# A trunk of two hybrid layers: three first projections taken by quarters of the adaLN weights, and the first GLA head drawn into the end of the RG-LRU

## The chip, the cores and the metric

The kernel runs on one core of a Trainium2 chip. The time is the device time of one execution in microseconds; of several executions the median counts.

## The reference

Two layers act on 512 tokens of 1024 features: 256 context tokens and 256 latent tokens. Both kinds share all weights. Only the latent stream is returned, so the second layer computes context rows only where latent rows read them. Each layer is, cut to what matters here:

```
mod   = c_silu @ mod_w + mod_b                  (shift, scale, gate; two of each)
h     = rms_norm(x, norm1_g) * (1 + scale) + shift
lx, ly, gq, gk, gv, gr, gz, aq, ak, av, bg = split(h @ w_in)
y1 = RG-LRU: conv of lx, gates a and i by tanh, a recurrence in both directions, times gelu(ly)
y2 = GLA:    4 heads, chunks of 64 tokens, decays from gz, both directions, rms norm, times silu(gr)
y3 = GQA:    8 heads over 2 key heads, rotary embedding, softmax
m  = sum over the branches of sigmoid(bg) * (y @ w_branch);  x = x + gate1 * (m @ w_out)
x  = x + gate2 * (relu(modulated norm of x @ mlp_w1) ** 2 @ mlp_w2)
```

## The kernel before

Features lie on the 128 partitions, eight k tiles of 128 of them, and tokens along the free axis. A weight tile is 128x1024 fp32 (512 KB). SP loads it into one of three buffers (`wraw`, L194), ACT casts it to a high part `wh` (L200), and DVE subtracts to get a low part `wl` (L201). The activations are split likewise into `hh` and `hl` (tile `h`, `split_to`, L293 and L294). A GEMM (`gemm`, L252) is 24 matmuls (L212): for each k tile wh by hh, wh by hl, and wl by hh. It sums in one of four PSUM banks named `mm`. Four other banks, `mx`, serve the small matmuls. In layer 1 GEMMs whose output is needed for the latent tokens only have 256 columns in place of 512 (`c0` is 256 there).

The program is written as one sequence, and a scheduler decides each engine's order from it. `tc.high_priority(AHEAD)` lets a weight's load and its two splits go ahead of their place. Each engine then works strictly in its own order, and the tables `LYS`, `MG`, `GZP` and `G0P` say after which step a piece of another branch is written.

**Beginning** (L438 to L475). The first four blocks of 2 MB of mod_w are quarters: each gives shift and scale for two k tiles. `mod_load` fetches a quarter in 16 pieces of 1 KB per partition. `mod_half` multiplies it with the conditioning vector (32 matmuls of L212, `mx<-modw,cs`), copies (L307), transposes (L216) and adds the bias (`modT`, L319). `norm_apply` makes the factor (`amul`, L420), multiplies (L425 on POOL, L427 on DVE), applies (L432 on DVE, L434 on ACT) and splits. After that stand nineteen small operations for the constants of RG-LRU (L454 to L475). Then come the GEMMs of ly (`gate_y`, three of them first) and of lx (`lru_conv`).

**RG-LRU** takes the eight blocks in pairs, i = 0, 2, 4, 6. `lru_conv` has a GEMM and four taps (L512 on ACT, L515 on DVE). `lru_gates` has four fp32 matmuls (L526) and tanh on ACT (L527, L531), and `lru_decay` an exp (L538). A square root over the pair (L630) needs another table on ACT. `lru_scan` has the recurrences on DVE (L545 to L555) and a split. After the pair i = 2, `gla_z` loads and splits `wz` and computes the decays' low rank input (L568, L572). After the pair i = 6, `gla_gates(0)` computes the decays of GLA's head 0 (L598 on PE; L601, L604, L605 on ACT with two table loads; L602 to L612 on DVE).

**GLA** takes four heads one after the other (`gla`, L648). A head computes its gates, k (copied out at L653), q (L656), for every second head v of two heads in four PSUM banks (L661), then for each direction `dd` the decayed k and q (L677 to L710), the scores (L715, L717), transposes of k (L728) and the states (L741), then the output (L760), its norm (L762 to L767), and r (two GEMMs, L769 to L772), whose product with the transposed output (L775, L776) is y2. Four `merge` steps of the first branch follow head 1 and four follow head 2. Then come GQA (k is transposed at L851), the other merges, the output projection and the MLP.

Of the kernel before, what the change touches and what calls it, by code (L numbers as in the profile page):

```python
# [15 lines left out]
F32 = mybir.dt.float32  # L16
# [7 lines left out]
KT = 8  # L24
# [6 lines left out]
WSPB, EBB, G2B, WRB = 3, 1, 3, 3  # L31
NSPL = 5
WQ = 1
# [4 lines left out]
GZP, G0P = 2, 6  # L38
# [66 lines left out]
def trunk_kernel(ctx: ExitStack, tc: tile.TileContext, out: bass.AP, d: dict):  # L105
# [48 lines left out]
    c8 = const.tile([128, KT, 2], F32, name="c8")  # L154
# [9 lines left out]
    pick = const.tile([128, 2, 32], F32, name="pick")  # L164
    G.memset(pick, 0.0)
    for b in range(2):
        G.memset(pick[:, b, b:b + 1], 1.0)
# [6 lines left out]
    th = const.tile([128, KT, 2], F32, name="th")  # L174
# [146 lines left out]
    def mods(l, us, pace, nd=KT):  # L321
# [19 lines left out]
        for u, j in halves:  # L341
            bs = (0, 1) if l == 0 or u < 2 else (1,)
            acc = [tmp() for _ in bs]
            terms = [(pick[:, b, :], a) for a, b in zip(acc, bs)]
# [22 lines left out]
    def mod_load(l, u, h, tag):  # L367

        t = yp.tile([128, KT, 2, 256], F32, name="modw", tag=tag)
        src = d["mod_w"][l, u]  # L370
        if u < 2:
            nc.sync.dma_start(t, src.rearrange("p k (h c) -> p k h c", h=2)[:, :, :, 256 * h:256 * h + 256])
        else:
            nc.sync.dma_start(t.rearrange("p k h c -> p k (h c)"), src[:, :, 512 * h:512 * h + 512])
        return t

    def mod_half(l, u, h, t):
        dsts = (4 * u + 2 * h, 8 + 4 * u + 2 * h) if u < 2 else (8 * u + 4 * h, 8 * u + 4 * h + 2)
# [759 lines left out]
```

## Time and profile before

| | |
|---|---|
| median of 3 runs | 1898.92 us (1896.93 to 1903.13) |
| the profiled execution | 1897.52 us, of which the span is 1895.7 |
| mean granted clock of TensorE | 0.989 |
| busy: PE, DVE, ACT, POOL | 1810.9, 1282.9, 924.8, 57.1 us |
| DMA | 255.62 MB, 135 GB/s in the mean |

The page gives the busy time of each engine first, then the span in 40 slices, the queues, the chain that ended last and the costliest groups of instructions. PE's digit falls below 9 in three places: the first slice, the fourth (142 to 190 us) and the 28th and 29th (1280 to 1374 us). Those places are looked at with the timeline and the waits.

### The profile page before, as it was taken

What the parts mean: (1) busy time and instruction counts of PE and PEld (TensorE: products, weight loads), DVE (VectorE), ACT (ScalarE), POOL (GpSimd) and SP (SyncE); (2) the same over time, 40 slices, a digit from 0 to 9 for tenths busy, and PEclk for the clock granted to TensorE, in tenths of its full rate; (3) what the DMA queues carried; (4) which work ended last, traced back from release to release, by engine and by line L of the source; (5) the groups of instructions that cost most, each with busy time, mean ns of one, the idle gap of its engine ahead of it and who ended that gap; (6) DMA issues with size and microseconds to landing.
All of it is one profiled execution on the core that took longest, in us unless ns stands there. A gap on an engine that the chain in (4) does not pass through costs nothing.

```text
span 1895.7 us, 26828 instructions
## 1 busy us (share of the span) xinstructions
PE 1810.9 (96%) x10248; PEld 1509.6 (80%) x10248; DVE 1282.9 (68%) x2177; ACT 924.8 (49%) x1586; POOL 57.1 (3%) x88
## 2 busy tenths in 40 slices
PE   5998999999999999999999999996999999999999
PEld 4765778887777888988888889764888878998887
DVE  5677764535566767789744448787765668577877
ACT  3778544334434333564232325876654554455443
POOL 1000000000000000000000001000000000000000
PEclk9999999999999999999999999998999999999999
DMA  9322223222211566666633335531343333664664
GB/s 318 99 74 73 69 69 90 77 93 78 72 51 56 190 193 196 222 224 199 211 109 97 98 102 185 164 114 61 130 122 111 122 123 91 234 193 150 190 190 154
DMA packets 91617, 255.62 MB, mean 135 GB/s; under 512 B 9184, under 2 KB 20576, under 8 KB 91488
## 3 DMA queue, kind: packets, MB, share of 16 engines
q1 hardware_dynamic: 91488, 253.90, 42.6%
q8 instruction: 81, 1.33, 0.3%
q14 instruction: 48, 0.39, 0.1%
HBM read 252.82 MB, written 1.05 MB: 134 GB/s over the span
## 4 chain that ended last, share of the span: by engine, by line
issue 49%; PE 39%; DVE 5%; ACT 4%; POOL 2%; DMA 0%; SPq 0%; POOLq 0%; ACTq 0%; DVEq 0%
PE mm L212 31%; PE mx L212 2%; PE mx L760 1%; PE mx L741 1%; DVE wl L201 1%; ACT wh L200 1%; PE mx L715 1%; PE mx L526 1%; POOL t L425 1%; PE mx L216 1%; DVE lru L546 0%; PE mx L717 0%; DVE lru L545 0%; ACT lru L630 0%; ACT lru L527 0%
## 5 line engine op out<-in xcount | busy, mean ns | idle before, releaser
L212 PE MATMUL mm<-h,wh 128*128 128x512 f32 (+1 forms) x2640 | 733.3, 360 | 8.3 <-DVE wh L198 4.5
L200 ACT CAST wh<-wraw 128x1024 fp32r<-128x1024 f32 x363 | 379.8, 1049 | 544.3 <-PE mm L212 465.3
L201 DVE TENSOR_TENSOR wl<-wraw,wh 128x1024 fp32r<-128x1024 f32 x365 | 445.8, 1223 | 257.6 <-ACT wh L200 254.2
L212 PEld LDWEIGHTS mm<-h,wh 128*128 128x128 f32 x2640 | 468.3, 189 | 85.4 <-issue 6.6
L212 PE MATMUL mm<-h,wl 128*128 128x512 f32 (+1 forms) x1448 | 493.2, 341 | 0.0
L212 PEld LDWEIGHTS mm<-h,wl 128*128 128x128 f32 x1448 | 273.8, 189 | 31.9 <-issue 1.4
L212 PE MATMUL mm<-yh,wh 128*128 128x512 f32 (+1 forms) x640 | 224.7, 351 | 2.4 <-DVE big L957 2.4
L212 PE MATMUL mm<-yh,wl 128*128 128x512 f32 (+1 forms) x640 | 224.3, 350 | 0.0
L212 PE MATMUL mm<-yl,wh 128*128 128x512 f32 (+1 forms) x640 | 222.6, 348 | 0.0
L212 PE MATMUL mm<-wh,h 128*128 128x512 f32 x576 | 187.3, 400 | 18.5 <-ACT t L653 18.1
L212 PE MATMUL mm<-yp,wh 128*128 128x256 f32 (+1 forms) x704 | 186.0, 338 | 3.8 <-ACT g L787 2.3
L212 PE MATMUL mm<-yp,wl 128*128 128x256 f32 x512 | 144.4, 282 | 0.0
L356 DVE SCALAR_TENSOR_TENSOR t<-t,cs,t 128x512 f32<-128x512 f32 x178 | 127.2, 746 | 24.1 <-DMA t<-mod_w 15.1
L212 PEld LDWEIGHTS mm<-wh,h 128*128 128x128 f32 x576 | 109.7, 191 | 42.3 <-ACT t L653 18.9
L212 PEld LDWEIGHTS mm<-yp,wh 128*128 128x128 f32 x704 | 120.8, 191 | 20.1 <-ACT g L787 2.5
L212 PEld LDWEIGHTS mm<-yh,wh 128*128 128x128 f32 x640 | 121.6, 190 | 17.8 <-issue 3.4
L212 PEld LDWEIGHTS mm<-yh,wl 128*128 128x128 f32 x640 | 121.2, 189 | 15.3 <-issue 0.7
L212 PEld LDWEIGHTS mm<-yl,wh 128*128 128x128 f32 x640 | 121.2, 189 | 15.0 <-issue 0.5
L212 PE MATMUL mm<-wl,h 128*128 128x512 f32 x288 | 115.2, 400 | 2.0 <-DVE wl L201 2.0
L212 PEld LDWEIGHTS mm<-yp,wl 128*128 128x128 f32 x512 | 97.1, 190 | 1.0 <-issue 1.0
L212 PE MATMUL mx<-t,t 128*128 128x128 f32 (+2 forms) x416 | 81.8, 338 | 0.0
L957 DVE SCALAR_TENSOR_TENSOR big<-mm,modT,big 128x256 f32<-128x256 f32 x64 | 28.6, 480 | 66.8 <-PE mm L212 66.8
(226 smaller groups left out, 1987.4 us busy)
## 6 DMA issues: line engine op xcount, KB each, us to landing
wraw<-wt SPq DMA_DIRECT2D x365, 512.0 KB, 3.6
t<-mod_w SPq DMA_DIRECT2D x144, 256.0 KB, 3.8
modw<-mod_w SPq DMA_DIRECT2D x6, 2048.0 KB, 14.1
big<-xt SPq DMA_DIRECT2D x8, 512.0 KB, 5.3
gw<-lruw SPq DMA_DIRECT2D x16, 256.0 KB, 3.5
out<-big SPq DMA_DIRECT2D x8, 128.0 KB, 2.5
t<-glaw SPq DMA_DIRECT2D x8, 96.0 KB, 3.1
t<-ropeg SPq DMA_DIRECT2D x2, 256.0 KB, 3.0
```

Source lines behind the costliest of these rows:

```text
L200: S.copy(wh, r)
L201: (G if lo == "G" else V).tensor_tensor(wl, r, wh.bitcast(F32), op=ALU.subtract)
L212: P.matmul(o, a, b, **kw)
L216: P.transpose(o, a, ident)
L356: V.scalar_tensor_tensor(a, t, c, a, op0=ALU.mult, op1=ALU.add)
L425: G.tensor_tensor(h[:, :n], x[:, k, c0:c1], st[1][:, :n], op=ALU.mult)
L526: P.matmul(pg, gw[:, 2 * dd + q, :], xc, start=True, stop=True)
L715: P.matmul(psc[:, c], en[:, c], em[:, c], start=True, stop=True)
L741: P.matmul(pu[:, :256], kt[:, 128 * t:128 * t + 128], v_[t], start=True, stop=True)
L760: P.matmul(po[:, :256], a, b, start=j == 0, stop=j == len(mm) - 1)
L957: V.scalar_tensor_tensor(x[:, i, c], ps[:, 256 * s - a:256 * s - a + 256], s0[:, i, s:s + 1], x[:, i, c], op0=ALU.mult, op1=ALU.add)
```

## The change

The four first quarters of mod_w (and the two that layer 1 loads at its end) are laid out on the host so that each is one row of 16 KB per partition, and the loads of the first two weights stand ahead of the third and after the first quarter. The first three ly projections (`first_gemm`) take the two k tiles of a quarter as soon as that quarter's norm is there, in three PSUM banks at once, between the multiplications of the next quarter. Their high parts are all cast by ACT. The RG-LRU constants are computed in `gate_consts` after the first `lru_conv`, in place where they can be. `wz` is loaded and split ahead of the RG-LRU loop, into the pool `g2`, which has four buffers in place of three.

In the last RG-LRU pair head 0's k and q GEMMs (`gla_kq`) come before the gates of block 6, and its decays and v (`gla_gates`, `gla_v`) between the gates of block 6 and of block 7. Its r GEMMs (`gla_r`) come before the last scans. For the other heads k and q come first, then the deferred end of the head before (`end`, transposes and product), then v and r. A head's state matmuls follow the k transposes of both directions. The end of head 3 comes after the attention's k and v projection.

```diff
...
-WSPB, EBB, G2B, WRB = 3, 1, 3, 3
+WSPB, EBB, G2B, WRB = 3, 1, 4, 3
...
-GZP, G0P = 2, 6
+GZP = 2
...
-                nc.sync.dma_start(t, d["mod_w"][l, u][:, k, 512 * j:512 * j + 512])
+                nc.sync.dma_start(t, d["mod_w"][l, u, j][:, k, :])
...
-        src = d["mod_w"][l, u]
-        if u < 2:
-            nc.sync.dma_start(t, src.rearrange("p k (h c) -> p k h c", h=2)[:, :, :, 256 * h:256 * h + 256])
-        else:
-            nc.sync.dma_start(t.rearrange("p k h c -> p k (h c)"), src[:, :, 512 * h:512 * h + 512])
+        nc.sync.dma_start(t, d["mod_w"][l, u, h].rearrange("p k (h c) -> p k h c", h=2))
...
-    mq = [mod_load(0, q // 2, q % 2, ("yh", "yl")[q % 2]) for q in range(WQ)]
-    first = [weight(0, "in", O_LY + 128 * i, hi="V", ahead=0) for i in range(2)]
-    mq += [mod_load(0, q // 2, q % 2, ("yh", "yl")[q % 2]) for q in range(WQ, 4)]
+    first = [weight(0, "in", O_LY + 128 * i, ahead=0) for i in range(2)]
+    mq = [mod_load(0, 0, 0, "yh")]
+    first.append(weight(0, "in", O_LY + 256, ahead=0))
+    mq += [mod_load(0, q // 2, q % 2, ("yh", "yl")[q % 2]) for q in range(1, 4)]
+    first_ps = [ps_mm.tile([128, 512], F32, name="mm") for _ in range(3)]
+    def first_gemm(i, q):
+        wh, wl = (a.rearrange("p (k m) -> p k m", k=8) for a in first[i])
+        for k in range(2 * q, 2 * q + 2):
+            mm(first_ps[i], wh[:, k, :], hn1[0][:, k, :], start=k == 0, stop=False)
+            mm(first_ps[i], wh[:, k, :], hn1[1][:, k, :], start=False, stop=False)
+            mm(first_ps[i], wl[:, k, :], hn1[0][:, k, :], start=False, stop=k == KT - 1)
     st = norm_stats(x1, 0)
     for q in range(4):
-        mod_half(0, q // 2, q % 2, mq[q])
+        for i in range(2) if q else ():
+            first_gemm(i, q - 1)
+        g = mod_half(0, q // 2, q % 2, mq[q])
+        next(g)
+        if q:
+            first_gemm(2, q - 1)
+        run(g)
         norm_apply(0, 1, x1, 0, T, st, hn1, range(2 * q, 2 * q + 2))
+    for i in range(3):
+        first_gemm(i, 3)
...
-    lo_, hi_ = PCOLS["lam"]
-    V.tensor_copy(lam, par[:, :, lo_:hi_])
-    S.activation(la, lam, AF.Abs)
...
-    V.tensor_scalar(c2[:, :, 0, :], lam, -4.0, None, op0=ALU.mult)
-    V.tensor_scalar(c2[:, :, 1, :], lam, 2.0, None, op0=ALU.mult)
...
-    V.tensor_scalar(habx, par[:, :, lo_:hi_], 0.5, None, op0=ALU.mult)
+    habx = par[:, :, lo_:hi_]
+    def gate_consts():
...
+        S.activation(la, lam, AF.Abs)
...
+        V.tensor_scalar(habx, habx, 0.5, None, op0=ALU.mult)
...
         def gate_y(i):
-            w = first[i] if l == 0 and i < 2 else weight(l, "in", O_LY + 128 * i, hi=E_LYH)
-            ps = gemm(w, hh, hl, c0)
+            if l == 0 and i < 3:
+                ps = first_ps[i]
+            else:
+                ps = gemm(weight(l, "in", O_LY + 128 * i, hi=E_LYH), hh, hl, c0)
...
+        wz = tmp1(F32, (128, KT, 32))
+        nc.sync.dma_start(wz, d["wz"][l])
+        wzs = g2.tile([128, KT, 64], F32R, name="wzs", tag="g2")
+        split_to(wzs[:, :, :32], wzs[:, :, 32:], wz)
...
-            wz = tmp1(F32, (128, KT, 32))
-            nc.sync.dma_start(wz, d["wz"][l])
-            wzs = t2.tile([128, KT, 64], F32R, name="wzs", tag="t2")
-            split_to(wzs[:, :, :32], wzs[:, :, 32:], wz)
...
+        v2 = {}
+        def gla_kq(h):
...
+            pk = gemm(weight(l, "in", O_GK + 128 * h), hh, hl, 0)
+            k_ = tmp()
+            cp(E_K)(k_, pk)
+            pq = gemm(weight(l, "in", O_GQ + 128 * h), hh, hl, c0)
+            q_ = tmp()
+            S.activation(q_[:, c0:], pq, AF.Copy, scale=128.0 ** -0.5)
+            return k_, q_
...
+        def gla_v(h):
...
+                for t, ps in gemm_tok(l, O_GV + 256 * h, hh, hl, range(4)).items():
...
+            return [v2.pop((h, t)) for t in range(4)]
...
+        def gla_r(h):
+            ys = []
...
+                pr = gemm(weight(l, "in", O_GR + 256 * h + 128 * j), hh, hl, c0)
+                y = gtmp()
+                S.activation(y[:, c0:], pr, AF.Tanh, scale=0.5)
+                V.scalar_tensor_tensor(y[:, c0:], y[:, c0:], 1.0, pr, op0=ALU.add, op1=ALU.mult)
+                ys.append(y)
+            return ys
...
         lru_conv(0)
+        if l == 0:
+            gate_consts()
         for i in range(0, 8, 2):
             lru_conv(i + 1)
-            lru_gates(i)
             if i < 6:
+                lru_gates(i)
                 lru_conv(i + 2)
+            else:
+                kq0 = gla_kq(0)
+                lru_gates(i)
+                gates0 = gla_gates(0)
+                v0 = gla_v(0)
             lru_gates(i + 1)
...
+            if i == 6:
+                ys0 = gla_r(0)
             for j in range(2):
                 lru_scan(i + j)
             if i == GZP:
                 zs = gla_z()
-            if i == G0P:
-                gates0 = gla_gates(0)
...
+        def gla(h, before=None):
+            if h:
+                bs = gla_gates(h)
+                k_, q_ = gla_kq(h)
+                before()
+                v_ = gla_v(h)
+                ys = gla_r(h)
+            else:
+                bs, (k_, q_), v_, ys = gates0, kq0, v0, ys0
...
-                kt = tmp()
+                kt = gtmp()
...
+                kts.append((kt, decp))
+            for dd, (kt, decp) in enumerate(kts):
+                seq = (0, 1, 2, 3) if dd == 0 else (1, 0, 3, 2)
...
-            for j in range(2):
-                pr = gemm(weight(l, "in", O_GR + 256 * h + 128 * j), hh, hl, c0)
...
-                V.scalar_tensor_tensor(y[:, c0:], y[:, c0:], 1.0, pr, op0=ALU.add, op1=ALU.mult)
-                po = mx()
...
+            def end():
+                for j, y in enumerate(ys):
+                    po = mx()
+                    for t in range(t0, 4):
+                        P.transpose(po[:, 128 * t:128 * t + 128], on[t - t0][:, 128 * j:128 * j + 128], ident)
+                    V.scalar_tensor_tensor(y[:, c0:], po[:, c0:], hg[:, j:j + 1], y[:, c0:],
+                                           op0=ALU.mult, op1=ALU.mult)
+                    split_to(y2h[:, 2 * h + j, c0:], y2l[:, 2 * h + j, c0:], y[:, c0:])
+            return end
...
+        end = None
         for h in range(4):
-            gla(h)
+            end = gla(h, end)
...
             av.append(a)
+        end()
...
-    a["mod_w"] = np.ascontiguousarray(mw.reshape(NL, 8, 128, 6, 1024).transpose(0, 3, 2, 1, 4))
+    mw = mw.reshape(NL, 8, 128, 6, 2, 512).transpose(0, 3, 4, 2, 1, 5).copy()
+    m0 = mw[0, :2].reshape(2, 2, 128, 8, 2, 256)
+    mw[0, :2] = m0.transpose(0, 4, 2, 3, 1, 5).reshape(2, 2, 128, 8, 512)
+    a["mod_w"] = mw
```

In these excerpts of the engines' orders "L212 MATMUL mx<-modw,cs" and its like are the line, the operation, and output and inputs. The number behind a name tells tiles apart. "x32" counts equal instructions in a row.

PE at the beginning, from the first quarter's multiplication on. Before (mm_444, mm_471 and mm_504 are the three ly projections):

```order
L212 MATMUL mx_195<-modw_129,cs_98 32x128 x32
L216 MATMUL mx_230<-ident_94,t1_228 128x128
L212 MATMUL mx_247<-modw_143,cs_98 32x128 x32
L212 MATMUL mm_444<-h_128,wh_133 128x512 x2
L216 MATMUL mx_282<-ident_94,t1_280 128x128
L212 MATMUL mm_444<-h_128,wl_134 128x512
L212 MATMUL mm_444<-h_128,wh_133 128x512 x2
L212 MATMUL mm_444<-h_128,wl_134 128x512
L212 MATMUL mm_471<-h_128,wh_139 128x512 x2
L212 MATMUL mm_471<-h_128,wl_140 128x512
```

With the change (mm_154, mm_155 and mm_156 are the three):

```order
L210 MATMUL mx_203<-modw_140,cs_98 32x128 x32
L214 MATMUL mx_238<-ident_94,t1_236 128x128
L210 MATMUL mm_154<-h_127,wh_130 128x512 x2
L210 MATMUL mm_154<-h_127,wl_131 128x512
L210 MATMUL mm_154<-h_127,wh_130 128x512 x2
L210 MATMUL mm_154<-h_127,wl_131 128x512
L210 MATMUL mm_155<-h_127,wh_136 128x512 x2
L210 MATMUL mm_155<-h_127,wl_137 128x512
L210 MATMUL mm_155<-h_127,wh_136 128x512 x2
L210 MATMUL mm_155<-h_127,wl_137 128x512
L210 MATMUL mx_267<-modw_148,cs_98 32x128 x32
L210 MATMUL mm_156<-h_127,wh_144 128x512 x2
```

The second quarter's multiplication stood ahead of the first projection, and now stands behind twelve matmuls of two projections.

ACT in layer 0 from the last exp of RG-LRU on, before (L630 is the square root, L601 to L605 are head 0's decays, L653 and L656 copy k and q):

```order
L538 ACTIVATE lru<-lru,c_403 128x512 x2
L630 ACT_TABLE_LOAD
L630 ACTIVATE lru<-lru,epsc 128x2048
L601 ACTIVATE eb<-mx,par 128x512 x2
L604 ACT_TABLE_LOAD
L604 ACTIVATE eb<-eb 128x1024
L605 ACT_TABLE_LOAD
L605 ACTIVATE eb<-eb 128x1024
L293 CAST yh<-lru 128x512
L653 COPY t_1323<-mm 128x512
L656 ACTIVATE t_1356<-mm 128x512
```

With the change, from block 6's gates on (L544 and L548 are tanh, L555 the exp of RG-LRU; L620 to L624 are head 0's decays):

```order
L544 ACTIVATE lru<-mx,par 128x512 x2
L548 ACTIVATE lru<-lru,c_483 128x512
L544 ACTIVATE lru<-mx,par 128x512 x2
L548 ACTIVATE lru<-lru,c_483 128x512
L620 ACTIVATE eb<-mx,par 128x512 x2
L555 ACT_TABLE_LOAD
L555 ACTIVATE lru<-lru,c_483 128x512
L623 ACTIVATE eb<-eb 128x1024
L198 CAST wh<-wraw 128x1024
L624 ACT_TABLE_LOAD
L624 ACTIVATE eb<-eb 128x1024
L555 ACT_TABLE_LOAD
```

The copy of k stood behind the square root, the decays and a split that takes the scan's result. Now the decays stand ahead of the square root, between the exps of blocks 6 and 7.

DVE in layer 1 at the scans of the last pair, before (L545 to L555):

```order
L545 SCALAR_TENSOR_TENSOR lru<-lru 128x512 x2
L546 TENSOR_TENSOR lru<-lru 128x512 x2
L548 SCALAR_TENSOR_TENSOR lru<-lru 128x512
L550 SCALAR_TENSOR_TENSOR lru<-lru 128x256
L545 SCALAR_TENSOR_TENSOR lru<-lru 128x512
L551 SCALAR_TENSOR_TENSOR lru<-lru 128x256
L546 TENSOR_TENSOR lru<-lru 128x512
L554 TENSOR_TENSOR lru<-lru 128x256
L548 SCALAR_TENSOR_TENSOR lru<-lru 128x512
L555 TENSOR_TENSOR lru<-lru,big 128x256
L545 SCALAR_TENSOR_TENSOR lru<-lru 128x512
L294 TENSOR_TENSOR yp<-lru,yp 128x256
```

With the change (the scans are L562 to L572, L199 splits weights, L663 is r's product):

```order
L562 SCALAR_TENSOR_TENSOR lru<-lru 128x512 x2
L199 TENSOR_TENSOR wl<-wraw,wh 128x1024
L563 TENSOR_TENSOR lru<-lru 128x512
L663 SCALAR_TENSOR_TENSOR g_10999<-g_10999,mm 128x256
L663 SCALAR_TENSOR_TENSOR g_11033<-g_11033,mm 128x256
L565 SCALAR_TENSOR_TENSOR lru<-lru 128x512
L199 TENSOR_TENSOR wl<-wraw,wh 128x1024
L563 TENSOR_TENSOR lru<-lru 128x512
L562 SCALAR_TENSOR_TENSOR lru<-lru 128x512
L567 SCALAR_TENSOR_TENSOR lru<-lru 128x256
L563 TENSOR_TENSOR lru<-lru 128x512
L199 TENSOR_TENSOR wl<-wraw,wh 128x1024
```

Weight splits and r's product now stand between the scans, where none stood before.

## Rows read from the trace of the kernel before

**Rows 1.** The page: busy time of each engine (share of the span) and instructions.
```profile
PE 1810.9 (96%) x10248; PEld 1509.6 (80%) x10248; DVE 1282.9 (68%) x2177; ACT 924.8 (49%) x1586; POOL 57.1 (3%) x88
```

**Rows 2.** Windows; columns: PE, PEld, DVE, ACT, POOL busy (count), PEclk, DMA share, GB/s.
```profile
100.00:200.00 100.00, 88.00 (x335) 62.83 (x333) 76.33 (x110) 72.28 (x91) 0.57 (x2) 0.95 0.21 67
1250.00:1350.00 100.00, 82.58 (x375) 59.68 (x374) 79.21 (x131) 66.22 (x100) 1.00 (x4) 0.91 0.32 100
1350.00:1400.00 50.00, 43.85 (x289) 39.64 (x289) 36.94 (x71) 27.57 (x55) 2.58 (x6) 0.93 0.37 118
```

**Rows 3.** PE's waits, whole span: us in total, times, longest us.
```profile
PE mm L212 <- ACT t L653: 19.6, 3, 10.4
...
PE mx L775 <- DVE t L767: 6.1, 8, 1.0
...
PE mx L526 <- DVE t L515: 4.1, 1, 4.1
...
PE mx L568 <- DVE wzs L294: 4.0, 2, 2.6
PE mx L715 <- DVE t L709: 3.7, 3, 1.3
PE mx L851 <- DVE t L841: 2.9, 2, 1.5
```

**Rows 4.** Timeline of PE, beginning; columns: start us, us, instruction [idle before <-releaser].
```profile
28.89 0.99 PE L212 MATMUL mm<-h,wh 128*128 128x512 f32 x2 [4.52 <-DVE wh L198]
...
37.03 0.39 PE L212 MATMUL mm<-h,wl 128*128 128x512 f32 x1
37.25 0.61 PE L212 MATMUL mm<-h,wh 128*128 128x512 f32 x2
...
38.02 1.95 PE L212 MATMUL mx<-modw,cs 128*32 128x128 f32 x64
...
43.43 0.97 PE L212 MATMUL mm<-h,wh 128*128 128x512 f32 x3 [1.97 <-ACT h L293]
```

**Rows 5.** Timeline of DVE, beginning.
```profile
21.39 1.18 DVE L464 TENSOR_SCALAR lc<-lc 128x32 f32<-128x32 f32 x1
...
24.70 0.22 DVE L319 TENSOR_TENSOR modT<-mx,par 128x4 f32<-128x4 f32 x2
```

**Rows 6.** Timeline of PE, end of layer 0's RG-LRU.
```profile
169.21 3.67 PE L526 MATMUL mx<-t,gw 128*128 128x512 f32 x8 [1.61 <-issue]
...
190.09 0.79 PE L212 MATMUL mm<-wh,h 128*128 128x512 f32 x1 [7.65 <-ACT t L653]
```

**Rows 7.** Timeline of ACT, end of layer 0's RG-LRU.
```profile
189.46 0.58 ACT L653 COPY t<-mm 128x512 f32<-128x512 f32 x1
```

**Rows 8.** Timeline of DVE, end of layer 0's RG-LRU, first and last scan rows.
```profile
180.54 1.29 DVE L545 SCALAR_TENSOR_TENSOR lru<-lru 128x512 f32<-128x512 f32 x2 [3.50 <-ACT lru L630]
...
198.41 0.68 DVE L294 TENSOR_TENSOR yl<-lru,yh 128x512 fp32r<-128x512 f32 x1
```

**Rows 9.** Timeline of PE, end of layer 1's RG-LRU.
```profile
1318.27 0.79 PE L212 MATMUL mm<-wh,h 128*128 128x512 f32 x1 [10.41 <-ACT t L653]
...
1319.29 1.05 PE L212 MATMUL mm<-wh,h 128*128 128x512 f32 x2
```

**Rows 10.** Timeline of DVE, end of layer 1's RG-LRU, first and last scan rows.
```profile
1309.47 1.29 DVE L545 SCALAR_TENSOR_TENSOR lru<-lru 128x512 f32<-128x512 f32 x2 [4.73 <-ACT lru L630]
...
1324.29 0.41 DVE L294 TENSOR_TENSOR yp<-lru,yp 128x256 fp32r<-128x256 f32 x1
...
1328.45 1.22 DVE L201 TENSOR_TENSOR wl<-wraw,wh 128x1024 fp32r<-128x1024 f32 x1
```

**Rows 11.** Timeline of ACT, end of layer 1's RG-LRU.
```profile
1304.62 1.51 ACT L538 ACTIVATE lru<-lru,c 128x512 f32<-128x512 f32 x2
1306.14 1.28 ACT L630 ACT_TABLE_LOAD   x1
1307.43 2.00 ACT L630 ACTIVATE lru<-lru,epsc 128x2048 f32<-128x2048 f32 x1
```

More of the change, by code (lines that the diff above doesn't have):

```diff
@@ L153, in trunk_kernel @@
     G.memset(cs, 0.0)
-    c8 = const.tile([128, KT, 2], F32, name="c8")
+    c8, th = (tmp1(shape=(128, KT, 2)) for _ in range(2))
     nc.sync.dma_start(c8, d["cs"])
@@ L161, in trunk_kernel @@
     G.memset(epsc, 1e-30)
-    pick = const.tile([128, 2, 32], F32, name="pick")
+    pick = const.tile([128, 33], F32, name="pick")
     G.memset(pick, 0.0)
-    for b in range(2):
-        G.memset(pick[:, b, b:b + 1], 1.0)
+    G.memset(pick[:, 1:2], 1.0)
     def pc(l, name, a=0, n=None):
@@ L343, in mods @@
             acc = [tmp() for _ in bs]
-            terms = [(pick[:, b, :], a) for a, b in zip(acc, bs)]
+            terms = [(pick[:, 1 - b:33 - b], a) for a, b in zip(acc, bs)]
             nx = load(u, j, 0)
@@ L378, in mod_half, with run @@
         dsts = (4 * u + 2 * h, 8 + 4 * u + 2 * h) if u < 2 else (8 * u + 4 * h, 8 * u + 4 * h + 2)
-        for _ in mod_cols(l, 128, lambda k: (cs[:, k, :], lambda c: t[:, k, c // 256, c % 256:c % 256 + 128]), KT,
-                          dsts):
+        return mod_cols(l, 128, lambda k: (cs[:, k, :], lambda c: t[:, k, c // 256, c % 256:c % 256 + 128]), KT, dsts)
+    def run(g):
+        for _ in g:
             pass
@@ L473, in trunk_kernel @@
     lo_, _ = PCOLS["ab"]
     _, hi_ = PCOLS["xb"]
-    V.tensor_scalar(habx, par[:, :, lo_:hi_], 0.5, None, op0=ALU.mult)
+    habx = par[:, :, lo_:hi_]
+    def gate_consts():
+        la, lb, lc = (tmp1(shape=(128, NL, 16)) for _ in range(3))
+        lo_, hi_ = PCOLS["lam"]
+        lam = par[:, :, lo_:hi_]
+        S.activation(la, lam, AF.Abs)
+        S.activation(la, la, AF.Exp, scale=-1.0)
+        V.tensor_scalar(lb, la, 2.0, None, op0=ALU.add)
+        V.reciprocal(lb, lb)
+        V.tensor_tensor(la, la, lb, op=ALU.mult)
+        V.tensor_tensor(lb, la, la, op=ALU.mult)
+        V.tensor_scalar(lc, lb, 1.0 / 17, 1.0 / 15, op0=ALU.mult, op1=ALU.add)
+        for n in (13, 11, 9, 7, 5, 3, 1):
+            V.tensor_tensor(lc, lc, lb, op=ALU.mult)
+            V.tensor_scalar(lc, lc, 1.0 / n, None, op0=ALU.add)
+        V.tensor_tensor(lc, lc, la, op=ALU.mult)
+        V.tensor_scalar(lam, lam, -1.0, 0.0, op0=ALU.mult, op1=ALU.max)
+        V.scalar_tensor_tensor(lam, lc, 2.0, lam, op0=ALU.mult, op1=ALU.add)
+        V.tensor_scalar(c2[:, :, 0, :], lam, -4.0, None, op0=ALU.mult)
+        V.tensor_scalar(c2[:, :, 1, :], lam, 2.0, None, op0=ALU.mult)
+        V.tensor_scalar(habx, habx, 0.5, None, op0=ALU.mult)
@@ L973, in trunk_kernel @@
             if last:
-                mod_half(l, 5, 0, mq[0])
+                run(mod_half(l, 5, 0, mq[0]))
             with tc.high_priority(NHP):
@@ L977, in trunk_kernel @@
             if last:
-                mod_half(l, 5, 1, mq[1])
+                run(mod_half(l, 5, 1, mq[1]))
                 done.add((l, 5))
```

47 lines of the change are left out of this document (6 added, 41 removed).

## The prediction

> **What bounds the kernel now.** The page first: PE is busy 96% of the span [rows 1], so a change can win only PE's idle time and its time at the lower clock. The windows show where these lie [rows 2]. From 100 to 200 us PE is idle 12.0 us at a granted clock of 0.95, which means some 10 us at 1.2 GHz instead of 2.4 (a microsecond at the lower level counts half in the mean). From 1250 to 1350 it is idle 17.4 us at 0.91 (18 us low), from 1350 to 1400 another 6.2 us at 0.93. These are the ends of RG-LRU in both layers. In the first two of these stretches DVE is busy 76 and 79% and ACT 72 and 66%, more than their 68% and 49% of the whole span, so cover is scarce in just these stretches. Then the list of PE's waits [rows 3]: the largest is v's GEMM, which needs a PSUM bank that the copy of k (L653) frees. Last the timelines: in layer 0 that copy runs at 189.46 [rows 7], behind a split that waits for the scans, and PE stood still for 7.65 us and resumed at 190.09 [rows 6]; in layer 1 it was 10.41 us [rows 9].
>
> **The sum, against the profiled 1897.52 us** (span 1895.7 and 1.8 around it; the median 1898.92 is 1.4 above it). No matmul, weight split or table load is added or dropped, so every term is a wait. On SP only the order changes (the second quarter ahead of the third weight, wz ahead of the first gates' weights), and PE's list of waits names no DMA, so I cost that at nothing. In the pool g2 the four buffers hold two products of r and two transposed k, which is what one head needs.
>
> *Beginning: 0.* Before, the first projection waited 4.52 us for a cast, and a later k tile 1.97 us [rows 4]. A part of the first wait goes with the constants, two of which took 1.2 us each [rows 5] ahead of the first modT at 24.70. But now the quarters form a chain. From the start of a quarter's multiplication (38.02) to its first projection (43.43) passed 5.4 us [rows 4], of which 1.95 are the multiplication. After it some 3.5 us of copy, transpose, modT, apply and split remain, and with the twelve matmuls (12 x 0.22 = 2.7 us, the step from 37.03 to 37.25) a cycle is near 10 us. Only the six matmuls of the third projection (1.4 us) cover the rest: two cycles lose some 3 us each and the last runs beside its predecessor. Against 6.5 us of old waits that is a draw. Ends: +4.5 if the cast's wait goes and nothing comes, -4 if a third cycle is exposed too. I take 0 because both sides come from the same rows. One-piece rows cost nothing and win nothing: the multiplication at 38.02 follows the projection's matmuls at 37.25 without an idle mark [rows 4], so PE's order and not the landing set its time. If that cover went, the first thing late would be the multiplication of the second quarter. The constants moved behind the first lx GEMM are some twenty small DVE operations, hidden under the GEMMs before the first gates, at worst about 4 us.
>
> *End of layer 0's RG-LRU: +14.* Of the 12.0 idle us, v's wait is 7.65, wzs 2.6 at most [rows 3] and the gates' matmuls 1.61 [rows 6]. The early split of wz takes 2.6 away, k and q ahead of block 6's gates cover the 1.61, and v ahead of the square root needs no bank behind the scans. At the lower clock PE loses at most half of 10 us, and I take 4, since most of that time follows those waits. Together 16. In exchange the decays' matmul waits for a bank that ACT's tanh frees, and ACT's in-order row has a split ahead that follows the scans of the pair before. No row shows it: ends 0 and 7.65, and I take 2, nearest to the 1.61 at the same place. The scans themselves (180.54 to 198.41 [rows 8]) now run beside r and the next head's k, q and r, some 33 us of GEMMs at 5.5 each, which hides them.
>
> *End of layer 1's RG-LRU: +6.* The same waits are 17.4 us idle and some 6 us of clock: 23.4, among them 10.41 for v and 4.1 for block 7's gates [rows 3, 9]. Here GEMMs with 256 columns take half as long, and the cover runs out. After the gates of block 7 ACT needs an exp pair, the table and the root, 1.5 + 1.3 + 2.0 us, with two tanh about 6.3 [rows 11]. Then DVE has the scans, 1309.47 to 1324.3 with small gaps [rows 10], and five weight splits of 1.22 now between them, some 22.5 us in all, and 3 us of the second direction's decays. That is 32 us until the second direction's scores. PE has only four r GEMMs and q at 2.8, k at 5.5 and small matmuls, about 21 us. It waits 11 us, and 2 more go to the lower clock after it. Head 1 then starts earlier than DVE and ACT can follow, for one eb buffer holds both directions: 4. So 23.4 - 11 - 2 - 4 = 6. Ends: -4 (weight splits late too) and +16 (only scans count, no splits between them).
>
> *The other heads: +8.* The transposes L775 waited 6.1 us in eight times, the scores 3.7, k's transposes in the attention 2.9 [rows 3], together 12.7. Now k and q stand ahead of the deferred transposes, r ahead of the scores, and the last head's end ahead of L851. I take 8: the scores still wait for the same decays on DVE. Ends 2 and 12.7.
>
> Sum 0 + 14 + 6 + 8 = 28: the profiled execution 1869.5, the median **1871 us**.
>
> **The rivals.**
> *Layer 1 gives all back.* DVE and ACT set the pace from the scans to head 1's end: its 6 become 0, half of layer 0's 14 and of the heads' 8 are lost: 11 gained, 1888 us. For it speaks the busy share of 79% on DVE [rows 2]; against it that layer 0's GEMMs are twice as long.
> *The cover holds.* The weight splits find gaps and the second direction waits for nothing: layer 1 gives 20, layer 0 16, the heads 10, the beginning 2, 48 in all, 1851 us. Against it stands DVE's order, in which the splits lie between the scans.
> *The clock is lost at the new waits.* After the 10.41 us wait the first matmul took 0.79 us, where 0.39 is usual [rows 4, 9]. If each of three quarters and of the two new waits in either layer brought PE to 1.2 GHz for its next matmuls, three quarters would cost up to 2.7 us each and four waits about 1 us more than I took: 12 us, 1883. The Trainium skill, "TensorE: Matmul & The Clock Gate", section "HAM oscillation — how this bites in real kernels", says that a loop whose short bursts alternate with waits falls back to the slow clock at every turn; by that rule the beginning by quarters is such a loop, and the rows of the beginning before, where the matmuls at 28.89 took 0.99 for two, agree with it for one wait.
> *Slower.* The weights of r, k and q pass DVE in order, and their splits stand between scans which wait for the root. If the GEMMs meant as cover so wait themselves, PE loses the whole 32 us in layer 1 in place of 11, and 15 in layer 0: 28 - 21 - 15 = -8, 1907 us. It decides from about 28 us of such waits beyond my 11; three buffers of each part, which let splits go two GEMMs ahead, speak against it.
> *The change does nothing.* Each wait removed comes back at the next instruction, as the two engines are full there: 1898 us.
>
> **How the numbers follow.** The forecast has 0.48 (its own range 1861 to 1881), layer 1 giving back 0.20, the cover holding 0.12, the clock 0.10, slower 0.06, nothing 0.04. About 0.3% (5.7 us) can be told from no change. Faster is 0.48 + 0.20 + 0.12 + 0.10 = 0.90, the same 0.04, slower 0.06. For 8 in 10 the range runs from 1852, which halves the case of the cover, to 1889, which takes in layer 1 giving back.
>
> **What would show it.** Right: v's wait behind L653 is gone in both layers; wzs waits nowhere; PE is nearly full from 100 to 200 us at a clock near 1; in layer 1 a wait of about 11 us stands at the second direction's scores (L767 in the new numbering) behind DVE; the third ly projection ends near the same time as before. Wrong: that wait under 3 us, or over 20 or in both layers; waits at r's or k's GEMMs for `wl`; a beginning that moves by more than 4 us.

## The result and the profile after

The changed kernel takes 1880.40 us (1879.06 to 1881.03) against 1900.49 (1896.93 to 1903.13) for the kernel before, four executions each: a ratio of 0.9895, interval 0.9875 to 0.9914. It is faster by about 20 us in the medians, some 1%, and the interval does not reach 1. The profiled execution took 1879.94 us, span 1878.2, which is 17.6 less than the profiled one before. The measured time lies inside the forecast range of 1852 to 1889 and 9 us above its 1871; the profile was forecast at 1869.5 and came out 10.4 above.

The page's first line answers to [rows 1]: the same matmuls, busy for as long, in a shorter span.

```profile
PE 1810.8 (96%) x10248; PEld 1518.2 (81%) x10248; DVE 1277.5 (68%) x2174; ACT 928.2 (49%) x1588; POOL 67.3 (4%) x87
```

The windows, with the columns of [rows 2]. The first row is the beginning before, the others are the changed kernel.

```profile
0.00:50.00 50.00, 28.94 (x331) 22.88 (x332) 27.48 (x76) 18.04 (x35) 6.98 (x17) 0.97 0.89 301
...
0.00:50.00 50.00, 27.91 (x312) 21.40 (x313) 20.79 (x45) 17.05 (x30) 8.95 (x16) 0.90 0.75 301
100.00:200.00 100.00, 97.14 (x380) 71.24 (x379) 74.29 (x104) 76.24 (x104) 0.32 (x1) 0.98 0.27 85
...
1250.00:1325.00 75.00, 73.89 (x392) 59.31 (x390) 62.12 (x93) 60.05 (x82) 2.93 (x3) 1.00 0.42 129
1325.00:1375.00 50.00, 29.73 (x162) 26.45 (x162) 35.76 (x75) 22.91 (x44) 1.96 (x6) 0.75 0.27 84
```

In layer 0 (100 to 200) 12.0 idle us became 2.9. In layer 1 the stretch up to 1325 is nearly full, and the 50 us behind it are only 29.73 us busy at 0.75, which is 25 us at the lower of the two clock levels (1.2 GHz of 2.4). That is as much as [rows 2] has for the end of layer 1 before (18 us and another 7). PE's waits of the whole span say who is late there (columns as in [rows 3]):

```profile
PE mx L767 <- DVE t L761: 13.9, 3, 9.6
...
PE mm L210 <- ACT h L291: 7.6, 3, 4.6
PE mx L767 <- DVE t L762: 4.8, 2, 3.8
...
PE mm L210 <- ACT t L641: 3.3, 1, 3.3
PE mx L617 <- ACT lru L544: 2.8, 1, 2.8
```

v's wait behind the copy of k (19.6 us in [rows 3]) and the wait for wzs are gone. New are the scores of head 0's second direction (9.6), head 1's scores behind it (3.8 and another of 3.6 in the 13.9), and the decays' matmul in layer 0 (2.8). The three waits for the first `h` (7.6) are the quarters.

To set each gain against its term, the span is cut where PE starts the gates of block 0 (the beginning ends), layer 0's attention transposes (its RG-LRU and GLA end), layer 1's gates of block 0, layer 1's attention transposes, and at the last matmul:

| us of stage | beginning | layer 0, RG-LRU and GLA | layer 0's rest and layer 1's start | layer 1, RG-LRU and GLA | rest |
|---|---|---|---|---|---|
| before | 65.12 | 411.10 | 724.17 | 328.65 | 362.53 |
| after | 69.30 | 393.05 | 726.90 | 322.31 | 362.43 |
| gained | -4.2 | +18.05 | -2.7 | +6.3 | +0.1 |
| in the forecast | 0 | 14 + most of 8 | 0 | 6 + the rest of 8 | 0 |

### The profile page after: what moved, and what is told of

The parts are those of the page before. It is cut to its first block, busy times and chain, and to the rows that moved or that the text cites. A ratio compares the mean times of both kernels' runs of the same rounds, so it can differ in the third digit from the quotient of the medians.

```text
span 1878.2 us, 26775 instructions
## 1 busy us (share of the span) xinstructions
PE 1810.8 (96%) x10248; PEld 1518.2 (81%) x10248; DVE 1277.5 (68%) x2174; ACT 928.2 (49%) x1588; POOL 67.3 (4%) x87
## 3 DMA queue, kind: packets, MB, share of 16 engines
HBM read 252.82 MB, written 1.05 MB: 135 GB/s over the span
## 5 line engine op out<-in xcount | busy, mean ns | idle before, releaser
L199 DVE TENSOR_TENSOR wl<-wraw,wh 128x1024 fp32r<-128x1024 f32 x365 | 445.3, 1222 | 245.2 <-ACT wh L198 238.0
```

The costliest lines, as they stand in the source:

```text
L199: (G if lo == "G" else V).tensor_tensor(wl, r, wh.bitcast(F32), op=ALU.subtract)
```

## The experiments

Three chips were used, one for the first four kernels, one for the next four and one for the last four, each time beside the kernel before, whose medians were 1900.9, 1902.2 and 1900.1. Stages are those of the table, from one profiled execution of each kernel. How far one execution can be trusted is seen where kernels share a stage. Layer 0's came out at 393.05, 393.05, 393.13, 393.11 and 392.85 for five kernels that do the same there, and layer 1's at 321.69 to 322.37 for five. The beginning is far less steady: the changed kernel's own code took 69.30 and 69.37 there, and in five of the kernels below that leave it as it is, 66.87, 68.68, 69.16, 69.36 and 69.87. The shortest and the longest of these (u_tail1 and s_late) have the same instructions on PE in the same order there, and their rows from 26 to 44 us differ in the granted clock (u_tail1 first):

```profile
26.00:44.00 18.00, 14.76 (x164) 10.92 (x165) 5.27 (x12) 4.22 (x8) 0.00 (x0) 0.88 0.76 304
26.00:44.00 18.00, 14.86 (x103) 10.35 (x107) 5.17 (x11) 3.96 (x7) 0.00 (x0) 0.70 0.76 303
```

PE is busy for as long in both. At 0.70 instead of 0.88 it is some 6.5 us longer at the lower level ((0.88 - 0.70) x 18 x 2), which costs up to 3.2 us and accounts for the 3.0 between the two.

**u_quarter** multiplies all quarters first and leaves the rest of the beginning as changed.

```diff
-        for i in range(2) if q else ():
-            first_gemm(i, q - 1)
-        g = mod_half(0, q // 2, q % 2, mq[q])
-        next(g)
-        if q:
-            first_gemm(2, q - 1)
-        run(g)
+        run(mod_half(0, q // 2, q % 2, mq[q]))
...
     for i in range(3):
-        first_gemm(i, 3)
+        for q in range(4):
+            first_gemm(i, q)
```

> The changed kernel, but the three first projections are written whole behind all four quarters, as before; layout, constants and everything later stay changed. Theory (the chain of quarters costs the beginning's 4.2 us, because the next quarter's multiplication stands behind twelve projection matmuls at the lower clock): block 0's gates start near 65 to 66 us instead of 69.30, time about 1876.5. Rival (the moved constants, the casts on ACT or the early wz cost it): gates still start near 69, time about 1880.4.

Measured: 1875.27 us (1874.41 to 1876.66), ratio 0.9868 (0.9853 to 0.9883), beginning 66.38. That is 2.9 us shorter than the changed kernel's, but only 0.5 below the shortest of the seven profiles of that code (66.87 to 69.87). So it is not shown that the interleaving as such costs. What is left of the changed beginning (rows in one piece, casts on ACT, constants later) is 1.3 us above the one profile before, which shows neither a gain nor a loss.

**b_first** keeps the quarters, but the multiplication of a quarter stands ahead of the projections of the quarter before, and the second quarter is loaded ahead of all weights.

```diff
-    first = [weight(0, "in", O_LY + 128 * i, ahead=0) for i in range(2)]
-    mq = [mod_load(0, 0, 0, "yh")]
-    first.append(weight(0, "in", O_LY + 256, ahead=0))
-    mq += [mod_load(0, q // 2, q % 2, ("yh", "yl")[q % 2]) for q in range(1, 4)]
+    mq = [mod_load(0, 0, q, ("yh", "yl")[q]) for q in range(2)]
+    first = [weight(0, "in", O_LY + 128 * i, ahead=0) for i in range(3)]
+    mq += [mod_load(0, 1, q, ("yh", "yl")[q]) for q in range(2)]
...
+        run(mod_half(0, q // 2, q % 2, mq[q]))
+        for i in range(3) if q else ():
             first_gemm(i, q - 1)
...
```

> The changed kernel, with the first quarters of mod_w loaded ahead of the three weights and a quarter's multiplication and transposes written ahead of the projections of the quarter before. Theory (what the chain needs is multiplications ahead of projections, and the one-piece rows make them land in time): the second quarter's multiplication starts near 22.5 us instead of 32.46, the gates of block 0 near 59 to 62 us instead of 69.30, time about 1871 to 1873. Rival (weights land later, so the first projection starts later by what the chain wins): gates at 66 or later, time 1878 or more.

The timeline of PE in the beginning of the changed kernel (columns as in [rows 4]):

```profile
17.95 3.64 PE L210 MATMUL mx<-modw,cs 128*32 128x128 f32 x64
...
26.90 1.52 PE L210 MATMUL mm<-h,wh 128*128 128x512 f32 x2 [4.59 <-ACT h L291]
...
31.20 1.05 PE L210 MATMUL mm<-h,wh 128*128 128x512 f32 x2
...
32.46 1.95 PE L210 MATMUL mx<-modw,cs 128*32 128x128 f32 x64
...
38.35 0.73 PE L210 MATMUL mm<-h,wh 128*128 128x512 f32 x2 [2.21 <-ACT h L291]
...
49.69 0.98 PE L210 MATMUL mm<-h,wh 128*128 128x512 f32 x3 [0.79 <-ACT h L291]
```

and of b_first:

```profile
17.99 3.64 PE L210 MATMUL mx<-modw,cs 128*32 128x128 f32 x64
...
22.28 1.96 PE L210 MATMUL mx<-modw,cs 128*32 128x128 f32 x64
...
26.45 1.96 PE L210 MATMUL mx<-modw,cs 128*32 128x128 f32 x64
...
30.34 0.73 PE L210 MATMUL mm<-h,wh 128*128 128x512 f32 x2 [1.94 <-ACT wh L198]
```

Measured: 1872.21 us (1871.45 to 1877.39), ratio 0.9857 (0.9838 to 0.9876), beginning 62.44: 6.9 us better than the change and 2.7 better than the one profile before. Three further kernels with this edit, best2, best3 and best4, have 62.00, 60.26 and 62.48, so all four lie 4.4 us or more below the seven with the changed kernel's beginning. The second multiplication starts at 22.28 instead of 32.46, so the copy, transpose, modT, apply and split of a quarter run while PE has other work. In the changed kernel two projections stand ahead of it, and they wait 4.59 us and then run with two matmuls in 1.05 us, where [rows 4] has 0.61: the twelve of them took 32.46 - 26.90 = 5.6 us. So the order was the fault, and quarters in the better order beat the whole projections of u_quarter. The edit moves loads and multiplications together, and the two were not tried apart; in the changed kernel's trace the second quarter has landed at 22.53, so its multiplication did not need an earlier load.

**u_end** writes a head's deferred transposes and product at once.

```diff
-            return end
+            end()
+            return lambda: None
```

> The changed kernel, but each head's end (transposes of the output and product) is written at the end of its own head again; r stays early. Theory (deferring the end is what removed the eight waits of L775, 6.1 us in all): those waits return with some 5 us, time about 1885. Rival (r's and k's early GEMMs cover them wherever the end stands): under 2 us of waits there, time about 1881.

Measured: 1888.07 us (1885.80 to 1890.28), ratio 0.9938 (0.9918 to 0.9958); layer 0's stage 398.99 (+5.9), layer 1's 323.95 (+1.6). So the deferral is worth 7.5 us in the stages, close to the 8 of the forecast. The waits at the transposes that come back are 2.8 us in three times in layer 0 and 2.7 in four in layer 1, the some 5 us of the theory; the other 2 of the 7.5 were not traced.

**s_late** writes layer 1's last two scans after head 0's second decays.

```diff
-            for j in range(2):
-                lru_scan(i + j)
+            if not last or i < 6:
+                for j in range(2):
+                    lru_scan(i + j)
...
                 kts.append((kt, decp))
+            if last and h == 0:
+                for j in range(2):
+                    lru_scan(6 + j)
+                y2.extend(ytiles("yl"))
...
```

> The changed kernel, but in layer 1 the scans of the last pair are written behind the decays and scores of both directions of head 0. Theory (the wait of 9.62 us before the second direction's scores is DVE's order, scans and splits ahead of the decays): that wait falls below 4 us, and the time to about 1874. Rival (DVE has as much to do in any order, and the wait comes back at head 1's k, q and scores or at the merges, which need the scans): the sum of PE's waits from 1250 to 1400 us stays near 22 us, time within 2 us of 1880.

Measured: 1874.07 us (1873.84 to 1880.47), ratio 0.9869 (0.9849 to 0.9890), layer 1's stage 321.08, only 1.2 better. PE's waits of s_late in its timeline, from the second direction's scores of head 0 (the first row) to those of head 1 (the last):

```profile
1324.55 0.71 PE L768 MATMUL mx<-t,t 128*128 128x128 f32 x4 [0.92 <-DVE t L763]
1332.16 1.22 PE L801 MATMUL mx<-t,g 128*128 128x256 f32 x2 [3.86 <-DVE t L806]
1335.66 5.32 PE L820 MATMUL mx<-t,t 128*128 128x256 f32 x12 [2.27 <-ACT yp L291]
...
1350.91 0.79 PE L210 MATMUL mm<-yp,wh 128*128 128x256 f32 x2 [3.29 <-ACT t L641]
1362.65 1.23 PE L768 MATMUL mx<-t,t 128*128 128x128 f32 x4 [4.23 <-DVE t L763]
1368.93 1.20 PE L768 MATMUL mx<-t,t 128*128 128x128 f32 x4 [3.60 <-DVE t L762]
```

The long wait fell from 9.62 to 0.92, so the theory was right on its cause, the order on DVE. In its place stand a wait of 3.86 for the update of the states on DVE (L806) and one of 2.27 that ends with the split of y1 (L291), and head 1's waits stay (3.29, 4.23 and 3.60, against 3.30, 3.76 and 3.60). All waits from 1250 to 1400 us sum to 19.2 us against 21.3, so the rival is mostly right about them: the new order moved most of what it removed. The better median does not speak against that: the three executions at 1874 were not profiled, and the profiled one took 1880.47 with the slower pace that the last section shows.

**after_ctl** is the changed kernel again, without an edit.

> The changed kernel once more, beside the others of this call. Theory (its executions spread little, and the clock after the wait at the start of layer 0's MLP is the only thing that differs): median 1879 to 1881, profile within 2 us of the first one. Rival (single executions of one kernel differ by up to 6 us, as in two of the runs before): one or more of the executions at 1874 to 1876 or at 1885.

Measured: 1879.00 us (1875.26 to 1880.00), ratio 0.9875 (0.9854 to 0.9896). One execution of four was at 1875.26: single executions of one kernel differ by several us, and medians of four that lie 3 us apart tell nothing. That is why the stages carry the argument below, those of the two layers above all.

**u_tail1** takes the overlap back in layer 1 alone: head 0's gates, k, q, v and r stand after the scans.

```diff
                 lru_conv(i + 2)
+            elif last:
+                lru_gates(i)
             else:
...
-            if i == 6:
+            if i == 6 and not last:
                 ys0 = gla_r(0)
...
+            if i == 6 and last:
+                gates0 = gla_gates(0)
+                kq0 = gla_kq(0)
+                v0 = gla_v(0)
+                ys0 = gla_r(0)
```

> The changed kernel, but layer 1 alone has the old order at the end of RG-LRU (block 6's and 7's gates, scans, then head 0's decays, k, q, v and r); the deferred ends stay. Theory (layer 1's overlap is worth about 5 us, what is left of over 20 us of removed waits): time 1885 to 1886, v's wait of about 10 us and the wait of 4 us at block 7's gates are back, the wait at the second direction's scores is gone. Rival (layer 1 gives all back): within 2 us of the changed kernel.

Measured: 1875.40 us (1870.44 to 1878.92), ratio 0.9858 (0.9832 to 0.9883); layer 1's stage 317.42. My theory was wrong: without the overlap the stage is 4.9 us shorter. Its waits from 1225 to 1400 us:

```profile
PE mm L210 <- ACT t L641: 11.8, 2, 10.3
PE mx L774 <- DVE t L768: 3.9, 1, 3.9
PE mx L774 <- DVE t L769: 1.3, 1, 1.3
```

v's wait of [rows 9] is back at 10.3, but the wait of 4 us at block 7's gates is not. These rows sum to 17.0 us where the changed kernel has 13.2 + 3.8 + 3.3 = 20.3 in the same window; with the short waits it is 20.2 against 21.8. Its windows:

```profile
1250.00:1325.00 75.00, 63.38 (x302) 48.30 (x300) 62.79 (x103) 55.29 (x80) 3.27 (x4) 0.93 0.31 102
1325.00:1375.00 50.00, 43.04 (x286) 39.21 (x285) 35.52 (x69) 27.21 (x54) 3.25 (x7) 0.93 0.35 114
```

PE is idle earlier and full later. Over the 125 us the clock is 0.93, where the changed kernel's two windows give (75 x 1.00 + 50 x 0.75) / 125 = 0.90. That is 17.5 us at the lower level against 25, worth up to 3.8 us. So of the 4.9 us the waits explain 1.6, and the clock at the new waits can explain the rest. best3, with the same layer 1, repeats the stage at 317.88.

**u_tail0** does the same to layer 0 alone.

```diff
...
+            elif not last:
+                lru_gates(i)
...
+            if i == 6 and (not last):
+                gates0 = gla_gates(0)
+                kq0 = gla_kq(0)
+                v0 = gla_v(0)
+                ys0 = gla_r(0)
```

> The changed kernel, but layer 0 alone has the old order at the end of RG-LRU, as u_tail1 had it in layer 1. There undoing the overlap won some 5 us. Theory (in layer 0 the GEMMs are twice as long and cover the scans, so here the overlap is worth what was forecast): v's wait of 7 to 8 us is back, head 1's first merges come 10 to 13 us later, time about 1891. Rival (the overlap gains nothing in layer 0 either; early r, the early wz and the deferred ends made the gain): within 3 us of 1880.

Measured: 1886.57 us (1881.56 to 1889.66), ratio 0.9925 (0.9903 to 0.9948); layer 0's stage 400.57, 7.5 longer. PE's waits from 100 to 300 us:

```profile
PE mx L543 <- issue: 4.0, 1, 4.0
PE mm L210 <- ACT t L641: 3.5, 1, 3.5
PE mx L617 <- DVE t L614: 1.0, 1, 1.0
```

and the window of [rows 2]:

```profile
100.00:200.00 100.00, 92.56 (x349) 66.75 (x348) 80.12 (x115) 77.07 (x98) 0.66 (x2) 0.95 0.21 69
```

Here the overlap wins, less than the theory said: v waits only 3.5 us without it, no longer the 7.65 of [rows 6], while the wait at the gates' matmuls, 1.61 there, is 4.0. PE is idle 7.4 us instead of 2.9, and some 10 us at the lower level instead of 4, worth up to 3 us. The same lines written into both layers gain 7.5 us where a GEMM has 512 columns and lose 4.9 where those of q and r have 256.

**g_early** writes the next head's decays ahead of the state matmuls, in both layers.

```diff
...
-                bs = gla_gates(h)
+                bs = nextg.pop()
...
                 kts.append((kt, decp))
+            if h < 3:
+                nextg.append(gla_gates(h + 1))
```

> The changed kernel, but the decays of the next head (gla_gates) are written before a head's state matmuls and output instead of behind them. Theory (head 1's waits in layer 1, 3.3 + 3.8 + 3.6 us, come from decays that start only when head 0's output is done, not from the one eb buffer): head 1's first scores in layer 1 start 8 to 12 us earlier than 1366.28, the three waits fall to under 5 us, time about 1873. Rival (DVE and ACT are full there, or the one eb buffer holds it): the waits move, time within 2 us of 1880.

Measured: 1880.80 us (1875.01 to 1881.78), ratio 0.9882 (0.9858 to 0.9905); layer 1's stage 318.37 (3.9 better), layer 0's 396.34 (3.3 worse). Head 1's first scores start at 1360.39 after a wait of 0.63, where the changed kernel had them at 1366.28 after 3.76, and the wait of 3.30 for the copy of k is gone too. Head 1's second direction still waits, 3.96 where it was 3.60, the long one of 9.6 stays, and layer 0 gives the gain back.

**u_wz** loads and splits wz inside `gla_z` again, in the pool `g2`.

```diff
-        wz = tmp1(F32, (128, KT, 32))
-        nc.sync.dma_start(wz, d["wz"][l])
-        wzs = g2.tile([128, KT, 64], F32R, name="wzs", tag="g2")
-        split_to(wzs[:, :, :32], wzs[:, :, 32:], wz)
...
         def gla_z():
...
+            wz = tmp1(F32, (128, KT, 32))
+            nc.sync.dma_start(wz, d["wz"][l])
+            wzs = g2.tile([128, KT, 64], F32R, name="wzs", tag="g2")
+            split_to(wzs[:, :, :32], wzs[:, :, 32:], wz)
```

> The changed kernel, but wz is loaded and split in gla_z again, in both layers, in the same pool. Theory (the early split takes away the waits of 2.6 and 1.4 us and the lower clock behind the first): time 1884 to 1885, gates after it in layer 0 some 3 to 4 us later. Rival (the moved split costs as much at the beginning as it wins): within 2 us of 1880.

Measured: 1877.36 us (1875.76 to 1879.37), ratio 0.9881 (0.9866 to 0.9896); layer 0's stage 391.49, 1.6 shorter. No wait for wzs returns, so loading it early removed nothing. Whether the old wait went with the other pool or with the new order around it was not separated.

**best2** has the edits of b_first, s_late and g_early together.

> The changed kernel with three edits together: quarters' loads and multiplications first (b_first), layer 1's last scans behind head 0's decays (s_late), the next head's decays early (g_early). Theory (the three act in different places): 8 + 3 + 7 us, time 1862 to 1864. Rival (s_late and g_early want the same DVE time): little more than b_first with one of them, 1867 to 1870.

Measured: 1870.18 us (1867.36 to 1871.30), ratio 0.9834 (0.9812 to 0.9856); beginning 62.00, layer 0 396.21 (g_early's loss), layer 1 317.80.

**best3** has the edits of b_first and u_tail1 together, and nothing else.

> The changed kernel with quarters' loads and multiplications first (b_first) and layer 1's old order at the end of RG-LRU (u_tail1). Theory (the two lie in different layers and add): 7 + 5 us, about 1867. Rival (the gain of u_tail1 was a difference between executions): 1872, as b_first.

Measured: 1865.57 us (1862.38 to 1868.63), ratio 0.9818 (0.9802 to 0.9834). Beginning 60.26, layer 0 392.86, layer 1 317.88: the two gains add. It is the best median of all kernels here, some 15 us below the change in the medians (1880.40 - 1865.57), which were measured on different chips.

**best4** adds to best3 g_early's edit for layer 1's head 1 alone.

```diff
...
+            if last and h == 0:
+                nextg.append(gla_gates(h + 1))
```

> best3, with the decays of head 1 in layer 1 written before head 0's state matmuls. Theory (with the old order DVE has room there, and the wait of 3.9 us at head 1's scores goes): 2 to 4 us below best3. Rival (as in g_early it is given back later): within 1 us of best3.

Measured: 1867.37 us (1864.47 to 1869.26), ratio 0.9827 (0.9812 to 0.9841). Layer 1's stage is 315.48, 2.4 better than best3's, but the median is not, and the intervals overlap. Whether it is worth anything stays open.

## Why the prediction was right, and where it was not

*The sign and the size.* Forecast 28, measured 17.6 in the profiles. Layers 0 and 1 up to the attention, where all 28 were, gave 18.05 + 6.3 = 24.4. The missing 10.4 are 3.6 there, 4.2 in the beginning and 2.7 in a stage without an edit, with 0.1 gained in the rest. Less than half of the 24.4 was taken apart by an experiment: the deferral 7.5, and the overlap 7.5 in layer 0 and -4.9 in layer 1. The other 14.3 lie in what those three kernels keep. So the sign is explained, but that the size came so near is in part luck: the overlap, priced at 14 and 6, fell short by 6.5 and 10.9, and most of that came back from parts that were not priced apart.

*Beginning, 0: off by 4.2, at its worse end.* More than 4 was one of the prediction's own signs of being wrong; other profiles of the same beginning are 1.8 to 4.8 us above the one before. "Two cycles lose some 3 us each and the last runs beside its predecessor" was right on the waits: 4.59, 2.21 and 0.79. It left out what follows the first of them. The rival of the clock was right for this place: after 4.59 idle us the matmuls ran at half pace and pushed the second multiplication to 32.46. The Trainium skill, "TensorE: Matmul & The Clock Gate", section "HAM oscillation — how this bites in real kernels", says that such a loop falls back to the slow clock at every turn. The trace agrees for two of the three turns: two matmuls take 1.05 us after the waits of 4.59 and 2.21, and three take 0.98 after the 0.79; the window's clock is 0.90 against 0.97. In u_tail1 the second wait is 2.21 as well, and two matmuls behind it take 0.62. My step also took PE's order as given and asked only what it costs; b_first shows that the same work in another order ends 6.9 us earlier, 4.4 at the least over all profiles. "One-piece rows cost nothing and win nothing" is not contradicted: the second quarter had landed at 22.29 us before and at 22.53 after, and its multiplication started at 38.02 and 32.46.

*End of layer 0, +14: right in its waits, too high for the overlap.* Gone are v's 7.65, the 1.61 and wzs; the decays' matmul waits 2.78 where I took 2, for the reason given. On ACT the split ahead of the block's activations waits for the pair before:

```profile
169.64 0.62 ACT L291 CAST yh<-lru 128x512 fp32r<-128x512 f32 x1 [3.55 <-DVE lru L572]
170.17 1.26 ACT L544 ACTIVATE lru<-mx,par 128x512 f32<-128x512 f32 x2
```

But the early wz was given 2.6 and brought nothing (u_wz: the wait stays away without it), and taking the overlap back costs 7.5. Of the stage's 18.05, 7.5 are the overlap's and 5.9 the deferral's, if the two are independent; some 4.7 lie in the other parts and were not separated.

*End of layer 1, +6: right in the wait, wrong in its worth.* The wait at the second direction's scores is 9.62 where I took 11, and DVE's row is the one foretold, scans with weight splits between them:

```profile
1312.48 1.29 DVE L562 SCALAR_TENSOR_TENSOR lru<-lru 128x512 f32<-128x512 f32 x2 [3.51 <-ACT lru L689]
1313.69 1.22 DVE L199 TENSOR_TENSOR wl<-wraw,wh 128x1024 fp32r<-128x1024 f32 x1
...
1327.44 1.20 DVE L199 TENSOR_TENSOR wl<-wraw,wh 128x1024 fp32r<-128x1024 f32 x1
...
1331.60 0.41 DVE L292 TENSOR_TENSOR yp<-lru,yp 128x256 fp32r<-128x256 f32 x1
...
1334.23 0.42 DVE L761 TENSOR_TENSOR t<-t,t 128x256 f32<-128x256 f32 x1
```

PE reaches those scores with its GEMMs done and stands still until 1334.71. The step that failed is "Head 1 then starts earlier than DVE and ACT can follow: 4". Head 1 measured 3.30 + 3.76 + 3.60 = 10.7 us of waits:

```profile
1353.80 0.80 PE L210 MATMUL mm<-yp,wh 128*128 128x256 f32 x2 [3.30 <-ACT t L641]
1366.28 0.76 PE L767 MATMUL mx<-t,t 128*128 128x128 f32 x4 [3.76 <-DVE t L762]
1372.09 1.19 PE L767 MATMUL mx<-t,t 128*128 128x128 f32 x4 [3.60 <-DVE t L761]
```

"2 more go to the lower clock" was too low as well: I counted 6 us of clock as won and 2 as lost again, and the 25 us at the lower level are as many as before. With the measured numbers my own sum becomes 17.4 - 9.6 - 10.7, which is -2.9. So the overlap, which I priced at about +6, is worth -4.9 (u_tail1). That the whole stage gained 6.3 beside a forecast of 6 is luck. The rival that layer 1 gives all back was right about this part and wrong about the stage: of its 6.3 the deferral is 1.6, and some 9.6 (6.3 - 1.6 + 4.9, if these are independent) come from what u_tail1 keeps, among it r's GEMMs ahead of the scores. The trace shows which waits u_tail1 lacks against before: 4.1 at block 7's gates, 2.3 at a merge and 1.4 for wzs. Which of the kept edits removed them was not tried.

*The other heads, +8: right as far as it was tried.* u_end measures 7.5 for the deferral. That k and q stand first and r ahead of the scores, which the same 8 covers, was not undone.

*The stage without an edit, -2.7.* Over the thirteen kernels other than before it was 723.5 to 727.9 us, against 724.17 before, and it does not follow the edits. In layer 0's MLP a wait of 2.36 us before and of 2.58 after stand at the same place; behind the first a matmul takes 0.28 us, behind the second 0.41 to 0.42. The first two rows are from before, the last two from after:

```profile
808.17 0.36 PE L212 MATMUL mm<-yh,wh 128*128 128x256 f32 x1 [2.36 <-DVE big L957]
808.36 0.28 PE L212 MATMUL mm<-yl,wh 128*128 128x256 f32 x1
...
793.97 0.55 PE L210 MATMUL mm<-yh,wh 128*128 128x256 f32 x1 [2.58 <-DVE big L1014]
794.32 0.42 PE L210 MATMUL mm<-yl,wh 128*128 128x256 f32 x1
```

From 785 to 800 us the changed kernel's granted clock is 0.78, some 6.6 us at the lower level, worth up to 3.3 us and so enough for the 2.7. Before it is 1.00 from 800 to 815. Why the clock fell behind one wait and not the other stays open; no edit stands there.

## What to carry to other kernels

Work drawn into another stage as cover can cost more than it hides: the same overlap won 7.5 us in the layer whose GEMMs have 512 columns and lost 4.9 in the one where many have 256, so test it in each layer by itself. (That the length of the GEMMs makes the difference is the likely reason; it was not tried alone.) When an input comes in pieces, put the small step that starts the long chain (here the next piece's multiplication) ahead of the bulk work that is meant to hide that chain. And after removing a wait, follow the waiting work into the next unit: in layer 1 the copy, decays and scores of the next head waited 10.7 us where the removed wait had been 10.41. Count the clock too: in layer 1 the waits moved, and 25 us at the lower level moved with them.

## What the runs showed of the hardware

Four multiplications on POOL took longer where DVE's first two weight splits ran beside them: in the changed kernel

```profile
21.08 1.24 DVE L199 TENSOR_TENSOR wl<-wraw,wh 128x1024 fp32r<-128x1024 f32 x1
...
23.39 1.21 DVE L199 TENSOR_TENSOR wl<-wraw,wh 128x1024 fp32r<-128x1024 f32 x1
...
18.73 7.00 POOL L422 TENSOR_TENSOR t<-big,t 128x512 f32<-128x512 f32 x4 [3.15 <-ACT t L402]
```

and in b_first, whose DVE had no split there (before, without one either, they took 4.97; in u_quarter and s_late, with the two, 7.01 and 7.00):

```profile
18.76 4.98 POOL L422 TENSOR_TENSOR t<-big,t 128x512 f32<-128x512 f32 x4 [3.16 <-ACT t L402]
```

And a PE that is busy throughout at a granted clock of 1.00 does not always keep the same pace. From 1750 to 1800 us, in layer 1's MLP, the changed kernel ran 291 matmuls and b_first 285:

```profile
1750.00:1800.00 50.00, 50.00 (x291) 44.10 (x290) 39.90 (x63) 23.67 (x35) 0.00 (x0) 1.00 0.63 190
```

```profile
1750.00:1800.00 50.00, 50.00 (x285) 43.36 (x284) 39.39 (x62) 23.55 (x34) 0.00 (x0) 1.00 0.61 186
```

Six of the fourteen profiled executions (b_first, s_late, g_early, u_tail0, u_wz and best4) had the slower pace, and their last stage took 365.4 to 366.1 us where the others took 361.6 to 362.7. No edit explains which; it is another 3 to 4 us by which two profiles can differ.
